# Rotary embedding and attention scores: a sixth load by GpSimd that leaves out four DMA engines, and fewer signals to TensorE

## The chip, the cores and the metric

The kernel runs on one core of one Trainium2 chip. The metric is the device time of an execution in microseconds (us). A core has five instruction streams: TensorE (PE, with its weight loads shown apart as PEld), VectorE (DVE), ScalarE (ACT), GpSimd (POOL) and SyncE (SP), and sixteen DMA engines, numbered 0 to 15 here, which carry every transfer between device memory and on-chip memory. A transfer is issued by SyncE, ScalarE or GpSimd and is spread over several of the sixteen by rows.

## The reference

Two inputs q and k of 16 batches, 512 positions, 16 heads and 64 numbers (32 MB each in fp32) are turned by a rotary embedding, and then all scores of a head are computed. The output has 16 x 512 x 16 x 512 numbers, 256 MB.

```python
q1, q2 = q[..., :half_dim], q[..., half_dim:]
q_rot = np.concatenate([q1 * cos_q - q2 * sin_q, q1 * sin_q + q2 * cos_q], axis=-1)
...
scores = np.einsum('bshd,bthd->bsht', q_rot, k_rot)
```

## The kernel before

A batch of q or k is one tile of 128 partitions: partition p holds positions 4p to 4p+3, which is one contiguous row of 16 KB, so a batch is 128 rows and 2 MB. There are two tiles for q and two for k (`ins`), used in turn. The work goes in 64 steps i (L394 for the first batch, L424 for the others); step i makes the scores of 128 positions of batch i // 4 against all 512 keys: eight pairs of heads, each two matmuls into one of three PSUM tiles `ps` (`scores`, L318), a copy by ScalarE into one of three stage buffers `st` of 4 MB, and one store of 4 MB by SyncE when the eight are there. Between them, TensorE transposes the next q and k parts into two PSUM tiles (`transposed`, L283), and VectorE does the rotary products (`rope_slot`, L251): sines, cosines, sum.

All order is written out by hand in a `Plan` (L11). For every operation it works out which semaphores its engine has to wait for. TensorE does not wait itself: each group of matmuls has a **relay** (L77), an instruction of GpSimd that waits for all that the group needs and then adds one to a semaphore of TensorE's (`emit_plain`, L465 to L476); the group waits for that count (`emit_group`, L487). A relay whose waits are all known already has none and is a bare signal (L475). TensorE's steps 4 to 59 are a loop of two steps (`emit_pe`, L492), whose semaphore is set back by the number of groups at the end of each step.

Loads: `load` (L215) fetches one batch of q or k. Most are issued by SyncE (L224) as one transfer of 128 rows; they stand in SyncE's queue between the stores. Five are in `RELIEVED` (L180) and go through `load_around` (L191): 120 rows by GpSimd in one transfer, the other 8 rows by GpSimd (for k) or by ScalarE (for q). GpSimd's transfers are put on consecutive engines from a cursor, and small copies into a scratch tile that nobody reads (`move_cursor`, L184) move it on by as many engines as they have rows. The relieved loads begin at engine 5 (`SLOW + 1`) and cover 15 engines, which leaves out engine 4. They stand in GpSimd's stream between the relays: a q load ahead of the first scores of its step (L432), a k load behind its step (L454). An input tile may be overwritten when VectorE's last product of the batch two before is done.

Of the kernel before, what the change touches and what calls it, by code (L numbers as in the profile page):

```python
# [7 lines left out]
PE, ACT, DVE, POOL, SP = "PE", "ACT", "DVE", "POOL", "SP"  # L8

class Plan:  # L11
# [7 lines left out]
    def __init__(self):  # L19
        self.ops = {e: [] for e in (PE, ACT, DVE, POOL, SP)}  # L20
        self.count = {}
        self.known = {e: {} for e in self.ops}
        self.writer = {}
        self.readers = {}
        self.phase = "start"
        self.relays = {}

    def _needs(self, reads, writes):
        need = {}
# [41 lines left out]
    def op(self, engine, emit, reads=(), writes=()):  # L71
        needs = self._needs(reads, writes)
        if engine == PE:
            waits = self._waits(POOL, needs, skip=(PE,))
            lane, n = self.phase, self.relays.get(self.phase, 0) + 1
            self.relays[lane] = n
            self.ops[POOL].append(("relay", waits, lane))  # L77
            for s, v in self.known[POOL].items():
                self.known[PE][s] = max(self.known[PE].get(s, 0), v)
            self.ops[PE].append(("group", (lane, n), emit))  # L80
        else:
            self.ops[engine].append(("op", self._waits(engine, needs), emit))
        self._done(engine, 1, engine, reads, writes)

    def dma(self, engine, lane, emit, reads=(), writes=()):
        waits = self._waits(engine, self._needs(reads, writes))
        self.ops[engine].append(("dma", waits, emit, lane))
        self._done(lane, 16, engine, reads, writes)

    def plain(self, engine, emit):  # L90
        self.ops[engine].append(("plain", [], emit))

    def enter(self, phase):

# [6 lines left out]
def kernel(  # L101
# [8 lines left out]
    nc = tc.nc  # L110
# [6 lines left out]
    P = 128  # L117
    C = S // P
# [3 lines left out]
    E = C * H * D  # L122
# [7 lines left out]
    dram = {  # L130
        "q": q.rearrange("b (p c) h d -> b p c h d", c=C),
        "k": k.rearrange("b (p c) h d -> b p c h d", c=C),
    }
# [7 lines left out]
    scratch = const_pool.tile([P, 96], fp32, name="scratch")  # L141
# [12 lines left out]
    plan = Plan()  # L154
# [5 lines left out]
    def dma(engine, lane, dst, src, reads=(), writes=()):  # L160
        plan.dma(engine, lane, lambda: engines[engine].dma_start(dst, src), reads, writes)  # L161
# [15 lines left out]
    def unit_keys(which, n):  # L177
        return [("unit", which, n, x) for x in range(2)]

    RELIEVED = {("q", 6): 0, ("k", 7): 1, ("q", 11): 2, ("k", 12): 3, ("q", 15): 4}  # L180
    SLOW = 4
    tiny = [0]

    def move_cursor(n):  # L184
        y = tiny[0]
        tiny[0] += 1
        src = bass.AP(q.tensor, 512 * y, [(512, n), (64, 2), (1, 2)])
        dst = scratch[:n, 4 * y : 4 * y + 4].rearrange("p (a b) -> p a b", a=2)
        dma(POOL, "tiny", dst, src, writes=[("scratch", y)])

    def load_around(which, b, t, keys):  # L191
        n, small = 120, E // 8
        x = RELIEVED[which, b]
        d = dram[which][b]

        def pieces(engine, lane, lo, hi, F):
            m = E // F
            src = bass.AP(d.tensor, d.offset + lo * E + E - F, [(E, hi - lo), (-F, m), (1, F)])
            v = t[lo:hi].rearrange("p c e -> p (c e)")
            dst = bass.AP(v.tensor, v.offset + E - F, [v.ap[0], (-F, m), (1, F)])  # L200
            dma(engine, lane, dst, src, writes=keys[lane[-1] == "r"])

        if x == 0:
            plan.plain(POOL, lambda: nc.gpsimd.inc_swdge_sem([], [], mode="reset_dge_cursor"))
        else:
            move_cursor(16 - SLOW)
        if x % 2:
            move_cursor(8)
            pieces(POOL, f"w{which}{b % 2}r", n, P, small)
        move_cursor(SLOW + 1)  # L210
        pieces(POOL, f"w{which}{b % 2}m", 0, n, E // 2)
        if not x % 2:
            pieces(ACT, f"a{which}{b % 2}r", n, P, small)

    def load(which, b):  # L215
        if b >= B:
            return
        t = ins[which][b % 2]
        keys = [[("in", which, b % 2, c, x) for c in range(C)] for x in range(2)]
        if (which, b) in RELIEVED:  # L220
            load_around(which, b, t, keys)
        else:
            dst = t.rearrange("p c (h d) -> p c h d", h=H)
            dma(SP, f"{which}{b % 2}m", dst, dram[which][b], writes=keys[0] + keys[1])  # L224

    def vec(out_ap, a, b, op, reads, writes):
        plan.op(DVE, lambda: nc.vector.tensor_tensor(out_ap, a, b, op=op), reads, writes)  # L227
# [23 lines left out]
    def rope_slot(which, n):  # L251
        c = n % C
        x = ins[which][n // C % 2][:, c]
        r = turned[which]
        cs = cos_t[:, c].unsqueeze(1).to_broadcast((P, 2 * H, HD))
        ss = ss_v[:, c].unsqueeze(1).to_broadcast((P, H, D))
        xs = x.rearrange("p (g j) -> p g j", j=D)
        xc = x.rearrange("p (g j) -> p g j", j=HD)
        x4 = x.rearrange("p (h x j) -> p h x j", x=2, j=HD)
        r4 = r.rearrange("p (h x j) -> p h x j", x=2, j=HD)  # L260
        swapped = bass.AP(r.tensor, r.offset + HD, [r.ap[0], (D, H), (-HD, 2), (1, HD)])
        ss4 = ss.rearrange("p h (x j) -> p h x j", x=2)
        u = [("in", which, n // C % 2, c, x) for x in range(2)]
        t = ("turned", which)

        def cosines():
            vec(xc, xc, cs, mult, [*u, "cos"], u)

        def sines():
            vec(swapped, x4, ss4, mult, [*u, "ss"], [t])  # L270

        def sums():
            vec(r4, x4, r4, add, [*u, t], [t])

        return [sines, cosines, sums]
# [79 lines left out]
    def run(ops):  # L355
        for op in ops:
            op()
# [36 lines left out]
    for i in range(C):  # L394
# [8 lines left out]
        for p in range(HP):  # L403
# [7 lines left out]
            if p in (2, 6):  # L411
                m = max(0, len(dve) - left[p == 6])
# [11 lines left out]
    for i in range(C, NST):  # L424
# [6 lines left out]
        q_ops = rope_slot("q", i + 2) if i + 2 < NST else []  # L431
        if i % C == C - 2 and ("q", i // C + 2) in RELIEVED:  # L432
            load("q", i // C + 2)
# [16 lines left out]
        if i % C == C - 2:  # L450
            if ("q", i // C + 2) not in RELIEVED:
                load("q", i // C + 2)
            if ("k", i // C + 3) in RELIEVED:
                load("k", i // C + 3)  # L454
# [5 lines left out]
    def sem(name):  # L460
        if name not in sems:
            sems[name] = nc.alloc_semaphore(name=f"s_{name}")
        return sems[name]

    def emit_plain(engine):  # L465
        eng = engines[engine]
        for item in plan.ops[engine]:
            kind, waits, fn = item[:3]
            if kind == "relay":
                for s, v in waits[:-1]:  # L470
                    eng.wait_ge(sem(s), v)
                if waits:
                    eng.wait_ge(sem(waits[-1][0]), waits[-1][1]).then_inc(sem(fn), 1)  # L473
                else:
                    eng.sem_inc(sem(fn), 1)  # L475
                continue  # L476
            for s, v in waits[:-1]:
                eng.wait_ge(sem(s), v)
            x = fn()
            if waits:  # L480
                x.wait_op(sem(waits[-1][0]), waits[-1][1], "sem-ge")
            if kind == "op":
                x.then_inc(sem(engine), 1)
            elif kind == "dma":
                x.then_inc(sem(item[3]), 16)

    def emit_group(relay, fn):  # L487
        xs = fn()
        xs[0].wait_op(sem(relay[0]), relay[1], "sem-ge")
        xs[-1].then_inc(sem(PE), 1)  # L490

    def emit_pe():  # L492
        ops = plan.ops[PE]
        turns = [x for x, o in enumerate(ops) if o[0] == "phase"]
        for o in ops[: turns[0]]:
            emit_group(*o[1:])
        nc.tensor.addr_align(256, max_nops=0)
        with nc.tensor.Fori(0, (len(turns) - 1) // UNROLL):
            for x in range(UNROLL):
                mine = ops[turns[x] + 1 : turns[x + 1]]  # L500
                for o in mine:
                    emit_group(*o[1:])
                lane = sem(f"turn{x}")
                nc.tensor.wait_ge(lane, len(mine)).then_inc(lane, -len(mine))
        for o in ops[turns[-1] + 1 :]:
            emit_group(*o[1:])

    with tc.tile_critical(no_gpsimd_drain=True):
        for engine in (SP, ACT, DVE, POOL):
            emit_plain(engine)  # L510
        for x in range(3):
            nc.sync.wait_ge(sem(f"st{x}"), plan.count[f"st{x}"])
        nc.gpsimd.wait_ge(sem("tiny"), plan.count["tiny"])
        nc.gpsimd.drain()
        emit_pe()

# [28 lines left out]
```

## Time and profile before

| | |
|---|---|
| median of 3 runs | 794.82 us (794.64 to 795.95) |
| the profiled execution | 793.15 us, its span 791.4 us |
| TensorE busy | 679.4 us, 86% of the span |
| VectorE, ScalarE busy | 573.9 us (73%), 552.1 us (70%) |
| DMA | 335.90 MB, mean 424 GB/s over the span |
| read, written | 67.24 MB, 268.44 MB |
| GpSimd's transfers | 3.1% of the DMA engines' time |
| stores of 4 MB, issue to landing | 25.4 us (60 of them) |
| relays with a wait, without | 626, 142 |

The span runs from the first to the last instruction. The time of a run lies a little above the span. A busy share is an average over the span; the slices of the page show how it is spread. A transfer's landing is signed off by sixteen records in the trace, one for each DMA engine, whether it carried data or not; the last of them lets the waiting instruction go.

### The profile page before, as it was taken

What the parts mean: (1) busy time and instruction counts of PE and PEld (TensorE: products, weight loads), DVE (VectorE), ACT (ScalarE), POOL (GpSimd) and SP (SyncE); (2) the same over time, 40 slices, a digit from 0 to 9 for tenths busy, and PEclk for the clock granted to TensorE, in tenths of its full rate; (3) what the DMA queues carried; (4) which work ended last, traced back from release to release, by engine and by line L of the source; (5) the groups of instructions that cost most, each with busy time, mean ns of one, the idle gap of its engine ahead of it and who ended that gap; (6) DMA issues with size and microseconds to landing.
All of it is one profiled execution on the core that took longest, in us unless ns stands there. A gap on an engine that the chain in (4) does not pass through costs nothing.

```text
span 791.4 us, 8521 instructions
## 1 busy us (share of the span) xinstructions
PE 679.4 (86%) x3072; PEld 290.4 (37%) x3072; DVE 573.9 (73%) x544; ACT 552.1 (70%) x647; POOL 11.9 (2%) x24
## 2 busy tenths in 40 slices
PE   4988999989978999698897978989889697999960
PEld 2443444333433434243343433334334243334320
DVE  7997898766857788585786767779578584877510
ACT  3978886866847777486684866868667685688770
POOL 0000000000010000000000001000000000000000
PEclk9999999988999999899998999999989998999995
DMA  9999999999999999999999999999999999999996
GB/s 354 421 425 439 428 436 434 421 441 432 428 428 434 427 431 410 442 429 429 433 431 434 431 428 434 428 429 417 440 426 432 437 428 428 435 432 428 435 434 270
DMA packets 19086, 335.90 MB, mean 424 GB/s; under 512 B 2376, under 2 KB 3656, under 8 KB 4936
## 3 DMA queue, kind: packets, MB, share of 16 engines
q1 hardware_dynamic: 16288, 324.61, 95.8%
q0 software_dynamic: 1872, 10.10, 3.1%
q10 hardware_dynamic: 904, 0.98, 0.4%
q14 instruction: 18, 0.15, 0.0%
q8 instruction: 4, 0.07, 0.0%
HBM read 67.24 MB, written 268.44 MB: 424 GB/s over the span
## 4 chain that ended last, share of the span: by engine, by line
DMA 48%; PE 29%; ACT 11%; DVE 7%; issue 0%; ACTq 0%; POOLq 0%; DVEq 0%; SPq 0%
DMA out_dram<-st 48%; PE ps L336 23%; ACT st L281 11%; PE bank L293 6%; DVE st L227 3%; DVE qr L227 2%; DVE kr L227 2%; DVE k_sb L227 1%; ACT kN L281 1%; DMA st<-in_k_dram 0%; DVE kT L279 0%; DVE q_sb L227 0%; ACTq L161 0%; POOLq L473 0%; ACTq L541 0%
## 5 line engine op out<-in xcount | busy, mean ns | idle before, releaser
L281 ACT COPY st<-ps 128x1024 f32<-128x1024 f32 x512 | 495.1, 1033 | 201.6 <-DMA out_dram<-st 132.2
L336 PE MATMUL ps<-kT,qT 64*128 64x512 f32 x1920 | 506.0, 646 | 71.7 <-POOLq L473 69.4
L336 PEld LDWEIGHTS ps<-kT,qT 64*128 64x128 f32 x1920 | 167.8, 194 | 252.8 <-POOLq L473 165.8
L279 DVE COPY qT<-bank 128x512 f32<-128x512 f32 x118 | 81.5, 691 | 115.0 <-PE bank L293 114.8
L227 DVE TENSOR_TENSOR kr<-k_sb,ss_t 128x1024 f32<-128x1024 f32 x60 | 73.2, 1220 | 27.1 <-PE bank L293 24.3
L293 PEld LDWEIGHTS bank<-ident,qr 128*128 128x128 f32 x480 | 52.6, 145 | 99.0 <-issue 66.2
L293 PEld LDWEIGHTS bank<-ident,kr 128*128 128x128 f32 x480 | 50.5, 141 | 94.7 <-issue 49.3
L293 PE MATMUL bank<-ident,qr 128*128 128x128 f32 x480 | 82.2, 296 | 1.3 <-POOLq L473 1.2
L293 PE MATMUL bank<-ident,kr 128*128 128x128 f32 x480 | 79.0, 288 | 2.1 <-POOLq L473 2.1
L281 ACT COPY kN<-bank 128x512 f32<-128x512 f32 x120 | 72.7, 608 | 8.5 <-PE bank L293 8.4
L227 DVE TENSOR_TENSOR qr<-q_sb,qr 128x1024 f32<-128x1024 f32 x60 | 73.5, 1225 | 2.0
L227 DVE TENSOR_TENSOR kr<-k_sb,kr 128x1024 f32<-128x1024 f32 x60 | 73.5, 1225 | 2.0
L227 DVE TENSOR_TENSOR q_sb<-q_sb,cos_t 128x1024 f32<-128x1024 f32 x60 | 73.5, 1225 | 2.0
L227 DVE TENSOR_TENSOR k_sb<-k_sb,cos_t 128x1024 f32<-128x1024 f32 x60 | 73.0, 1216 | 0.2
L227 DVE TENSOR_TENSOR qr<-q_sb,ss_t 128x1024 f32<-128x1024 f32 x60 | 72.9, 1216 | 0.0
L279 DVE COPY kT<-kN 128x2048 f32<-128x2048 f32 x28 | 34.3, 1226 | 30.4 <-PE ps L336 18.6
L293 PE MATMUL bank<-ident,st 128*128 128x128 f32 x64 | 10.7, 317 | 12.2 <-POOLq L473 12.2
L336 PE MATMUL ps<-kN,qT 64*128 64x512 f32 x64 | 16.7, 643 | 0.0
L336 PE MATMUL ps<-kN,st 64*128 64x512 f32 x64 | 16.3, 616 | 0.0
L161 POOL DMA_DIRECT2D scratch<-in_q_dram x11 | 6.3, 575 | 631.5 <-DVE qT L279 613.8
L293 PEld LDWEIGHTS bank<-ident,st 128*128 128x128 f32 x64 | 8.3, 161 | 17.4 <-POOLq L473 17.4
L227 DVE TENSOR_TENSOR qr<-st,ss_t 128x1024 f32<-128x1024 f32 x8 | 9.8, 1221 | 5.4 <-DMA st<-in_k_dram 5.3
(19 smaller groups left out, 50.6 us busy)
## 6 DMA issues: line engine op xcount, KB each, us to landing
out_dram<-st SPq DMA_DIRECT2D x60, 4096.0 KB, 25.4
k_sb<-in_k_dram SPq DMA_DIRECT2D x13, 2048.0 KB, 30.0
q_sb<-in_q_dram SPq DMA_DIRECT2D x12, 2048.0 KB, 28.7
out_dram<-st SPq DMA_DIRECT2D x16, 1024.0 KB, 14.0
q_sb<-in_q_dram POOLq DMA_DIRECT2D x3, 1920.0 KB, 28.2
k_sb<-in_k_dram POOLq DMA_DIRECT2D x2, 1920.0 KB, 50.8
st<-in_k_dram SPq DMA_DIRECT2D x1, 1536.0 KB, 8.9
st<-in_q_dram SPq DMA_DIRECT2D x1, 1536.0 KB, 11.9
```

Source lines behind the costliest of these rows:

```text
L161: plan.dma(engine, lane, lambda: engines[engine].dma_start(dst, src), reads, writes)
L227: plan.op(DVE, lambda: nc.vector.tensor_tensor(out_ap, a, b, op=op), reads, writes)
L279: plan.op(DVE, lambda: nc.vector.tensor_copy(out=dst, in_=src), reads, writes)
L281: plan.op(ACT, lambda: nc.scalar.copy(out=dst, in_=src), reads, writes)
L293: return [nc.tensor.transpose(bank[:, x, :], srcs[x], ident) for x in range(4)]
L336: nc.tensor.matmul(out=ps[:, r, :], lhsT=lhs[64 * r : 64 * r + 64, :], rhs=rhs[64 * r : 64 * r + 64, :], start=True, stop=True,)
```

## The change

Two things are changed.

First, q of batch 13 joins the relieved loads, with another split (`MORE`): 24 rows, then 96 rows, both by GpSimd and counted by the code as twelve engines from engine 5 on (5 to 15 and 0), then 8 rows by GpSimd from engine 8 on. Its rows have three keys and three semaphores instead of two. The copies that move the cursor are now worked out from where the code believes the cursor to be (`cursor[0]`), each transfer adding the number of engines that is written beside it: 15, 12 or 8. So the other relieved loads are led by one or two small copies instead of up to three.

Second, the plan notes whether GpSimd has waited for anything since its last relay (`heard`). A relay that has no wait, and before which GpSimd heard nothing new, is dropped (`thin`), and its group on TensorE waits for no count. The counts of the others are numbered anew. Where a relay has several waits, two go into one instruction.

```diff
+            self.ops[POOL].append(("relay", waits, lane, n, bool(waits) or self.heard))
+            self.heard = False
...
+    def thin(self):
+        needed = {o[2:4] for o in self.ops[POOL] if o[0] == "relay" and o[4]}
+        rank, count = {}, {}
+        for place in sorted(needed):
+            lane = place[0]
+            count[lane] = rank[place] = count.get(lane, 0) + 1
+        self.ops[POOL] = [o for o in self.ops[POOL] if o[0] != "relay" or o[2:4] in needed]
+        self.ops[PE] = [
+            ("group", (o[1][0], rank.get(o[1])), o[2]) if o[0] == "group" else o for o in self.ops[PE]
+        ]
+        return count
...
-    RELIEVED = {("q", 6): 0, ("k", 7): 1, ("q", 11): 2, ("k", 12): 3, ("q", 15): 4}
     SLOW = 4
+    ONE, MORE = 15, 12
+    RELIEVED = {("q", 6): ONE, ("k", 7): ONE, ("q", 11): ONE, ("k", 12): ONE, ("q", 13): MORE, ("q", 15): ONE}
+    cursor = [None, 0]
+
+    def move_cursor(to):
+        if cursor[0] is None:
+            plan.plain(POOL, lambda: nc.gpsimd.inc_swdge_sem([], [], mode="reset_dge_cursor"))
+            cursor[0] = 0
+        n, y = (to - cursor[0]) % 16, cursor[1]
+        if n:
+            src = bass.AP(q.tensor, 512 * y, [(512, n), (64, 2), (1, 2)])
+            dst = scratch[:n, 4 * y : 4 * y + 4].rearrange("p (a b) -> p a b", a=2)
+            dma(POOL, "tiny", dst, src, writes=[("scratch", y)])
+            cursor[:] = [to, y + 1]
...
+        def pieces(engine, lane, lo, hi, F, written, first=None, n=0):
...
+            if engine == POOL:
+                move_cursor(first)
+                cursor[0] = (first + n) % 16
+            dma(engine, lane, dst, src, writes=written)
+
+        x = b % 2
+        if RELIEVED[which, b] == MORE:
+            pieces(POOL, f"w{which}{x}r", 96, 120, wide, keys[1], SLOW + 1, MORE)
+            pieces(POOL, f"w{which}{x}m", 0, 96, wide, keys[0], SLOW + 1, MORE)
+            pieces(POOL, f"w{which}{x}s", 120, P, small, keys[2], 8, 8)
+        elif which == "k":
+            pieces(POOL, f"w{which}{x}r", 120, P, small, keys[1] + keys[2], 8, 8)
+            pieces(POOL, f"w{which}{x}m", 0, 120, wide, keys[0], SLOW + 1, ONE)
+        else:
+            pieces(POOL, f"w{which}{x}m", 0, 120, wide, keys[0], SLOW + 1, ONE)
+            pieces(ACT, f"a{which}{x}r", 120, P, small, keys[1] + keys[2])
...
     def emit_group(relay, fn):
         xs = fn()
-        xs[0].wait_op(sem(relay[0]), relay[1], "sem-ge")
+        if relay[1]:
+            xs[0].wait_op(sem(relay[0]), relay[1], "sem-ge")
         xs[-1].then_inc(sem(PE), 1)
...
-                nc.tensor.wait_ge(lane, len(mine)).then_inc(lane, -len(mine))
+                n = count[f"turn{x}"]
+                nc.tensor.wait_ge(lane, n).then_inc(lane, -n)
```

The new `load_around` gives GpSimd's pieces of q of batch 13 with `wide` = 2048 numbers and `small` = 512 numbers as the length of one run in a row; rows are the slowest dimension on both sides of every one of these transfers.

More of the change, by code (lines that the diff above doesn't have):

```diff
@@ L76, in op @@
             self.relays[lane] = n
-            self.ops[POOL].append(("relay", waits, lane))
+            self.ops[POOL].append(("relay", waits, lane, n, bool(waits) or self.heard))
+            self.heard = False
             for s, v in self.known[POOL].items():
@@ L81, in op @@
         else:
-            self.ops[engine].append(("op", self._waits(engine, needs), emit))
+            waits = self._waits(engine, needs)
+            self.heard |= engine == POOL and bool(waits)
+            self.ops[engine].append(("op", waits, emit))
         self._done(engine, 1, engine, reads, writes)
@@ L86, in dma @@
         waits = self._waits(engine, self._needs(reads, writes))
+        self.heard |= engine == POOL and bool(waits)
         self.ops[engine].append(("dma", waits, emit, lane))
@@ L178, in unit_keys @@
         return [("unit", which, n, x) for x in range(2)]
-    RELIEVED = {("q", 6): 0, ("k", 7): 1, ("q", 11): 2, ("k", 12): 3, ("q", 15): 4}
     SLOW = 4
[L182 to L189, printed above, removed]
+    ONE, MORE = 15, 12
[11 more added lines that the diff above has]
+            cursor[:] = [to, y + 1]
     def load_around(which, b, t, keys):
-        n, small = 120, E // 8
-        x = RELIEVED[which, b]
+        wide, small = E // 2, E // 8
         d = dram[which][b]
-        def pieces(engine, lane, lo, hi, F):
+        def pieces(engine, lane, lo, hi, F, written, first=None, n=0):
             m = E // F
@@ L200, in pieces @@
             dst = bass.AP(v.tensor, v.offset + E - F, [v.ap[0], (-F, m), (1, F)])
-            dma(engine, lane, dst, src, writes=keys[lane[-1] == "r"])
-        if x == 0:
-            plan.plain(POOL, lambda: nc.gpsimd.inc_swdge_sem([], [], mode="reset_dge_cursor"))
-        else:
[L206 to L213, printed above, removed]
+            if engine == POOL:
[10 more added lines that the diff above has]
+            pieces(POOL, f"w{which}{x}m", 0, 120, wide, keys[0], SLOW + 1, ONE)
+        else:
+            pieces(POOL, f"w{which}{x}m", 0, 120, wide, keys[0], SLOW + 1, ONE)
+            pieces(ACT, f"a{which}{x}r", 120, P, small, keys[1] + keys[2])
     def load(which, b):
@@ L218, in load @@
         t = ins[which][b % 2]
-        keys = [[("in", which, b % 2, c, x) for c in range(C)] for x in range(2)]
+        keys = [[("in", which, b % 2, c, x) for c in range(C)] for x in range(3)]
         if (which, b) in RELIEVED:
@@ L223, in load @@
             dst = t.rearrange("p c (h d) -> p c h d", h=H)
-            dma(SP, f"{which}{b % 2}m", dst, dram[which][b], writes=keys[0] + keys[1])
+            dma(SP, f"{which}{b % 2}m", dst, dram[which][b], writes=keys[0] + keys[1] + keys[2])
     def vec(out_ap, a, b, op, reads, writes):
@@ L262, in rope_slot @@
         ss4 = ss.rearrange("p h (x j) -> p h x j", x=2)
-        u = [("in", which, n // C % 2, c, x) for x in range(2)]
+        u = [("in", which, n // C % 2, c, x) for x in range(3)]
         t = ("turned", which)
@@ L469, in emit_plain @@
             if kind == "relay":
[L470 to L475, printed above, removed]
+                if not waits:
+                    eng.sem_inc(sem(fn), 1)
+                while waits:
+                    now, waits = waits[:2], waits[2:]
+                    x = eng.wait_ge(sem(now[0][0]), now[0][1])
+                    if len(now) == 2:
+                        x.wait_op(sem(now[1][0]), now[1][1], "sem-ge")
+                    if not waits:
+                        x.then_inc(sem(fn), 1)
                 continue
@@ L488, in emit_group, with emit_pe @@
         xs = fn()
-        xs[0].wait_op(sem(relay[0]), relay[1], "sem-ge")
+        if relay[1]:
+            xs[0].wait_op(sem(relay[0]), relay[1], "sem-ge")
         xs[-1].then_inc(sem(PE), 1)
-    def emit_pe():
+    def emit_pe(count):
         ops = plan.ops[PE]
@@ L503, in emit_pe @@
                 lane = sem(f"turn{x}")
-                nc.tensor.wait_ge(lane, len(mine)).then_inc(lane, -len(mine))
+                n = count[f"turn{x}"]
+                nc.tensor.wait_ge(lane, n).then_inc(lane, -n)
         for o in ops[turns[-1] + 1 :]:
             emit_group(*o[1:])
+    relayed = plan.thin()
     with tc.tile_critical(no_gpsimd_drain=True):
@@ L514 @@
         nc.gpsimd.drain()
-        emit_pe()
+        emit_pe(relayed)
 _INS = ['q', 'k', 'cos', 'sin']
```

## The prediction

> **What bounds the kernel now.** I read the page's slices first, then the chain, then the end of the span in short stretches, then what GpSimd waits for. From the page's second part (40 slices, busy share in tenths, and GB/s) and its fourth (the chain that ended last):
>
> ```profile
> DMA  9999999999999999999999999999999999999996
> GB/s 354 421 425 439 428 436 434 421 441 432 428 428 434 427 431 410 442 429 429 433 431 434 431 428 434 428 429 417 440 426 432 437 428 428 435 432 428 435 434 270
> DMA 48%; PE 29%; ACT 11%; DVE 7%; issue 0%; ACTq 0%; POOLq 0%; DVEq 0%; SPq 0%
> ```
>
> The DMA engines are full from the first slice to the last but one, which no compute engine is (TensorE 86%). The chain's 29% of TensorE misleads: it runs under a full queue. Summed over the trace's packet records, the sixteen engines are idle for 0.6 us per engine before 780 us, 0.5 of it in the first 10 us. So waits of TensorE, ScalarE or GpSimd cost nothing as long as the queue holds work. Only the last slice is not full. Its stretches (columns: busy time of PE, PEld, DVE, ACT, POOL, granted clock, DMA share, GB/s):
>
> ```profile
> 770.00:780.00 10.00, 0.00 (x0) 0.00 (x0) 0.00 (x0) 0.00 (x0) 0.00 (x0) 0.57 1.02 439
> 780.00:782.00 2.00, 0.00 (x0) 0.00 (x0) 0.00 (x0) 0.00 (x0) 0.00 (x0) 0.50 0.80 344
> 782.00:784.00 2.00, 0.00 (x0) 0.00 (x0) 0.00 (x0) 0.00 (x0) 0.00 (x0) 0.50 0.57 246
> 784.00:786.00 2.00, 0.00 (x0) 0.00 (x0) 0.00 (x0) 0.00 (x0) 0.00 (x0) 0.50 0.42 180
> 786.00:788.00 2.00, 0.00 (x0) 0.00 (x0) 0.00 (x0) 0.00 (x0) 0.00 (x0) 0.50 0.11 49
> 788.00:791.40 3.40, 0.00 (x0) 0.00 (x0) 0.00 (x0) 0.00 (x0) 0.00 (x0) 0.50 0.02 10
> ```
>
> All compute is over; the sixteen engines run out one after another, and the last one sets the time. Which one? Every transfer leaves sixteen landing records. Those of the last store, in us behind the first (781.85), are 0, 0.33, 0.34, 0.43, 1.57, 1.62, 1.85, 1.92, 1.96, 3.05, 4.70, 4.98, 5.40, 5.60, 7.64, 8.15. Their mean is 3.1: bytes moved between engines can win at most 8.15 - 3.1 = 5 us.
>
> To name the engines I followed packets: on one engine the next packet starts 3 to 4 ns before the last one's end. The 8-row pieces that ScalarE issues touch eight engines (I number them 0 to 7), those of GpSimd the other eight, 8 to 15. Of the two small copies at 656 us, with twelve and five rows, exactly one engine carries both, so the second begins where the first came round: 4 to 15, then 0 to 4. That sorts the list: **engine 4** 8.15; engines 0 to 3: 1.85, 5.40, 5.60, 7.64 (I take 1.85 for engine 0, the one that no 8 KB instruction fetch was seen to hit); 5 to 7: 1.92, 1.96, 4.98; 8 to 15: 0, 0.33, 0.34, 0.43, 1.57, 1.62, 3.05, 4.70. Engine 4 is last for a reason: until 767 us its 32 KB packets take a median 1255 ns, the others' 1213, so it loses 0.33 us per 4 MB store. Only the five loads by GpSimd, which leave it out, hold it back:
>
> ```profile
> q_sb<-in_q_dram POOLq DMA_DIRECT2D x3, 1920.0 KB, 28.2
> k_sb<-in_k_dram POOLq DMA_DIRECT2D x2, 1920.0 KB, 50.8
> scratch<-in_q_dram POOLq DMA_DIRECT2D x5, 0.1 KB, 7.6
> scratch<-in_q_dram POOLq DMA_DIRECT2D x4, 0.2 KB, 13.3
> ```
>
> In the landings of each of these five loads one engine comes 3.8 to 5.9 us ahead of fifteen: the one with nothing to carry. The scratch rows are the small copies that turn GpSimd's cursor.
>
> **The change, part by part.**
>
> *Signals left out.* The trace has 142 signals without a wait:
>
> ```profile
> L475 POOLq EVENT_SEMAPHORE  x142: 17/17/17, 9.3 to 758.7; - x142
> PEld ps L336 <- POOLq L475: 2.3, 9, 0.5
> POOL q_sb L161 <- DVE qr L227: 17.3, 3, 5.9
> ```
>
> At most these 142 go, 142 x 17 ns = 2.4 us of GpSimd's sequencer, and TensorE waited 2.3 us for them. The DMA queue hides both: 0. Without that cover it would be 2.3 us. Putting two waits into one instruction changes nothing: 112 of the 626 waiting signals already carry two. Fewer instructions are fewer fetches: 18 packets of 8 KB (0.31 us each) for the 2255 instructions of all engines but TensorE is 65 bytes each, so 142 spare about 1.1 packets, 0.35 us on one engine. I take 0 and keep -0.35 for the range. Small copies go from 11 to 10, with packets of 9 ns: 0.
>
> *The load moved to GpSimd.* q of batch 13 leaves SyncE's queue (issued at 575.08) and goes into GpSimd's before step 46, so it waits for VectorE's last product of step 45 with TensorE's signals of step 46 queued behind it. The row is the same kind of load at step 54: copies at 656.07, 5.68 us of waiting, load at 662.87. Step 45's store left SyncE at 559.11 where step 53's left at 658.80, so the copies would come near 556.4 and the load near 563.2, with three pieces (0.75, 0.75, 0.59) and three copies (0.56 each): 3.8 us more at most. TensorE stands for 5.7 to 9.5 us. What hides it: store 46 waits anyway for its buffer, whose last store lands at 565.3; and from its issue at 574.70 to its first landing, 592.90, lie 18.2 us, of which 9.7 are its own service (one store to the next at the end, 772.20 to 781.85). So 8.5 us are queue. Price 0; with all of 9.5 uncovered, 1.0 us dry. The removed issue on SyncE (0.85) and VectorE's waits for three lanes in place of one (17 ns each, as a signal of GpSimd's) are 0 as well.
>
> *Where the bytes go.* This decides. A row is 16 KB, 0.61 us (611 ns in one packet, 2 x 309 in two). Before, q of batch 13 put eight rows on every engine. The new pieces have 24, 96 and 8 rows, and the code counts the first two as twelve engines each. The trace has no GpSimd transfer of 96 rows. It shows 120 rows on 15 engines, 12 on 12, 8 on 8, 5 on 5, and SyncE's 128 rows on 16: each time the largest number up to 16 that divides the rows; for 120 not 12 or 10, though both divide. By these rows 24 goes on 12, but **96 goes on 16**, six rows each. That is the value I take; the other bound is the code's 12, eight rows each.
>
> The Trainium skill, "DMA: Bandwidth & Descriptors", section "Why a DMA increments its semaphore by 16 and not by 1", says the same of the rule: the largest k up to 16 that divides both sides' slowest dimension, all engines at k = 16, otherwise k consecutive ones from a cursor. The trace agrees on 120, 12, 8 and 5; no run here shows 96. By that page the sum is the one that follows; by the code's count it is the first rival's.
>
> With 16, the count slips. After the 24 rows (engines 5 to 15 and 0) the cursor is at 1; a copy of four brings it to 5; the 96 rows go everywhere and leave it at 5, while the code believes 1. Its copy of seven leads to 12, not 8: the 8 rows fall on 12 to 15 and 0 to 3, and the cursor ends at 4, not 0. Before the last load (q of batch 15) the code moves by five, to 9, not 5: its 15 engines are 9 to 15 and 0 to 7. **It leaves out engine 8 and gives engine 4 eight rows.**
>
> Sum for engine 4: batch 13, 6 - 8 = -2 rows, -1.2; batch 15, 8 instead of 0, +4.9; 8.15 - 1.2 + 4.9 = 11.85, so +3.7 us. No other comes near: 7.64 - 0.6 = 7.0 (engines 1 to 3, 7 rows); 4.70 + 0.6 = 5.3 (12 to 15, 9 rows).
>
> *Slow reads behind such loads.* In the first SyncE load after each pair of GpSimd loads, 16 KB reads took up to 1.72 us instead of 0.61 (300 to 308 us; again 541 to 555); mean lateness rose by 0.6 and 0.5 us, the latest engine's by 1.8 and 0.1. The k load at 590.84 would now follow one. Whether it pays is open: 0 taken (a single load comes before it, not a pair), 1.8 kept for the range.
>
> The profiled execution took 793.15 us with a span of 791.4, 1.75 around it; the median of the runs is 794.82, 1.67 higher. Span 791.4 + 3.7 = 795.1; on the median 794.82 + 3.7 = **798.5 us**. The runs lie from 794.64 to 795.95, so the case's own range is 797.2 (less the fetch and a spread of 0.9) to 800.3 (plus 1.8).
>
> **Rivals.**
>
> *The 96 rows do use twelve engines.* Engines 1 to 4 get nothing: 7.64, 5.60, 5.40 and 8.15 fall by 4.9, to 3.3 and less. Engines 8 to 15 get 11 rows, +1.8: 4.70 becomes 6.5; engines 5 to 7 get 10: 4.98 becomes 6.2. The end moves from 8.15 to 6.5, -1.6 us: 793.2. For it: it is just what would relieve the four latest. Against: the 120-row rows.
>
> *Sixteen engines, but the cursor comes out where the code believes.* The last load then spares engine 4: 8.15 - 1.2 = 6.9, 793.6. Against: nothing shows a transfer on sixteen moving the cursor by twelve.
>
> *Twelve engines, and step 46 runs the queue dry.* 1.0 us dry and 0.6 of slow reads give the gain back: 794.8. It decides only once TensorE's stand exceeds 8.5 us; the three waits behind VectorE were at most 5.9 each.
>
> *Engine 4 does not matter.* The same page of the Trainium skill (section "Latency and other measured facts") says engines 7 and 15 are usually the slower, with SWDGE's rings as the guess. Worked out here: if 4.98 and 8.15 were swapped, engine 7 at 8.15 would get 6 + 2 rows and its usual eight at batch 15, and the time would stay 794.8. The trace disagrees: the engine with 1255 ns packets carries rows of both small copies, and it is slow long before GpSimd's first load (from some 50 us).
>
> **How the numbers follow.** Forecast 0.71; twelve engines 0.18; cursor right 0.04; dry queue 0.05; engine 7 0.02. A measurement tells some 0.2% from no change, 1.6 us: below 793.2 faster, above 796.4 slower. Twelve engines lie on that bound: 0.11 faster, 0.07 same; cursor right 0.02 and 0.02; the last two same. Faster 0.13, same 0.16, slower 0.71. The forecast's own range holds some 0.64; to reach 0.8 the range goes down over the middle cases to 793.1.
>
> **What would show it.** In the landings of q of batch 13's 96-row piece, four early engines mean twelve, none means sixteen. In the last load, the engine left out must be one with 1213 ns packets. The last store's landings should end 11.8 behind the first, by the engine with 1255 ns packets, with the next near 7, and DMA still full before 780 us. I am wrong if four engines come early, or if an idle stretch of the DMA opens near 575 to 600 us.

## The result and the profile after

| | before | after |
|---|---|---|
| median | 794.73 us (4 runs, 793.30 to 795.95) | 802.73 us (4 runs, 801.93 to 804.19) |
| ratio, with its 95% interval | | 1.0103 (1.0079 to 1.0128) |
| the profiled execution, its span | 793.15, 791.4 us | 804.19, 802.4 us |
| idle time of one DMA engine, mean of the sixteen | 5.5 us | 12.5 us |
| GpSimd's transfers, share of the DMA engines | 3.1% | 3.7% |

The kernel became slower, as forecast, but by 8.0 us and not by 3.7, and 802.73 us lies above the stated range. The two profiled executions lie 11.0 us apart, more than the medians: the one of before is low among its runs, the one of after is the highest of its four.

First the slices and the chain of the changed kernel's page, to be held against those of before:

```profile
DMA  9999999999999999999999999999999999999994
GB/s 346 421 426 432 440 387 425 429 429 441 423 432 430 426 438 412 433 437 429 431 428 440 433 428 425 422 431 423 432 426 411 428 430 434 419 407 422 436 425 178
DMA 53%; PE 24%; ACT 12%; DVE 6%; issue 1%; POOL 0%; ACTq 0%; POOLq 0%; DVEq 0%; SPq 0%
```

The last slice holds 178 GB/s where it held 270, slices 35 and 36 (some 680 to 720 us) fall to 419 and 407, and slice 6 (100 to 120 us) to 387. Those are the three places where most of the time went; a fourth, smaller one is slice 31 (some 600 to 620 us, behind the sixth load), 411 where before has 432. The end, in short stretches (some of the rows; columns as before, the last two are DMA share and GB/s):

```profile
780.00:782.00 2.00, 0.00 (x0) 0.00 (x0) 0.00 (x0) 0.00 (x0) 0.00 (x0) 0.56 1.22 524
788.00:790.00 2.00, 0.00 (x0) 0.00 (x0) 0.00 (x0) 0.00 (x0) 0.00 (x0) 0.50 0.76 328
790.00:792.00 2.00, 0.00 (x0) 0.00 (x0) 0.00 (x0) 0.00 (x0) 0.00 (x0) 0.50 0.19 82
792.00:794.00 2.00, 0.00 (x0) 0.00 (x0) 0.00 (x0) 0.00 (x0) 0.00 (x0) 0.50 0.08 33
794.00:796.00 2.00, 0.00 (x0) 0.00 (x0) 0.00 (x0) 0.00 (x0) 0.00 (x0) 0.50 0.08 33
796.00:798.00 2.00, 0.00 (x0) 0.00 (x0) 0.00 (x0) 0.00 (x0) 0.00 (x0) 0.50 0.04 16
798.00:800.00 2.00, 0.00 (x0) 0.00 (x0) 0.00 (x0) 0.00 (x0) 0.00 (x0) 0.50 0.08 33
```

Two packets of 32 KB in 2 us make 33 GB/s, one makes 16. So from 792.8 us on a single engine works, for 8 us. In the landings of the last store fifteen engines come within 2.55 us of the first (790.26), and engine 4 comes 10.79 behind it. Before, the sixteen were strung out over 8.15 us with a mean of 3.1. Engine 4 no longer is the last of a crowd: it alone carries more.

How long it had been so shows in the stores from 640 us on. These are from the landing records of the changed kernel (us; the last columns are the latest and the next latest engine behind the first):

```
issued   first landing   latest   next
647.22   660.42          11.10    6.39
657.23   674.98          15.21    8.17
667.24   687.24          14.67    8.36
683.55   699.37          12.54    6.46
699.57   710.46          11.48    5.02
710.36   721.24          10.73    3.91
720.37   731.25          10.73    3.55
730.40   741.29          10.68    3.16
```

The latest engine was 15 us behind at 675 us. A stage buffer is free only when the last of its sixteen records is there, so the others then began to wait for engine 4, and the stores fell into its pace: 10.0 us from one to the next (721.24 to 731.25), eight packets of 1255 ns, where before they came every 9.7, eight of 1213 ns. That is the dip at 680 to 720. It shows as missing GB/s while TensorE is nearly full, in the changed kernel:

```profile
690.00:700.00 10.00, 8.67 (x34) 3.62 (x36) 5.56 (x6) 8.60 (x10) 0.00 (x0) 0.83 0.94 400
720.00:730.00 10.00, 10.00 (x50) 4.34 (x48) 8.44 (x9) 8.37 (x11) 0.00 (x0) 1.00 0.99 426
730.00:740.00 10.00, 10.00 (x50) 4.33 (x48) 6.74 (x7) 8.38 (x11) 0.00 (x0) 1.00 0.97 416
```

and in the kernel before, in the same stretches:

```profile
690.00:700.00 10.00, 9.12 (x44) 3.78 (x44) 7.56 (x8) 7.96 (x10) 0.00 (x0) 1.00 1.01 436
720.00:730.00 10.00, 10.00 (x50) 4.41 (x50) 6.76 (x7) 8.59 (x11) 0.00 (x0) 1.00 1.02 440
730.00:740.00 10.00, 9.81 (x46) 4.01 (x46) 6.46 (x8) 7.92 (x9) 0.00 (x0) 1.00 1.01 434
```

Summed over the packet records, the 11.0 us of the profiled pair come out so. Idle time per engine behind 780 us rose by 4.6 (4.9 to 9.5), before it by 2.4 (1.9 of it between 690 and 750 us). Packets that took longer than the usual 1213, 611 or 309 ns cost 3.8 us per engine more (3.8 to 7.6), 1.8 of it at 100 to 120 us, long before the first load that the change touches; such a patch stands there in some executions of the kernels below and not in others. Together 10.8. The idle time fits the late engine; that the slow packets have to do with the change is not shown.

Where did engine 4 fall behind? Followed packet by packet, it is +1.1 us against before at 470 us, +8.4 at 550, +7.3 at 656, +11.1 at 700, and +11.05 at the end. **The largest step, 7.3 us, falls on the time of q of batch 11 and k of batch 12**, two loads that were relieved before as well, and the next, 3.8 us, on q of batch 15. Over the time of the new load 1.1 us came back. In that first stretch engine 4 carries no 8 KB packet for GpSimd before, and 32 of them after: eight rows of each of the two loads.

### The profile page after: what moved, and what is told of

Read it like the earlier page. It is cut to its first block, busy times and chain, and to the rows that moved or that the text cites. A ratio compares the mean times of both kernels' runs of the same rounds, so it can differ in the third digit from the quotient of the medians.

```text
span 802.4 us, 8390 instructions
## 1 busy us (share of the span) xinstructions
PE 680.4 (85%) x3072; PEld 291.8 (36%) x3072; DVE 573.3 (71%) x544; ACT 551.6 (69%) x647; POOL 13.4 (2%) x26
## 4 chain that ended last, share of the span: by engine, by line
DMA 53%; PE 24%; ACT 12%; DVE 6%; issue 1%; POOL 0%; ACTq 0%; POOLq 0%; DVEq 0%; SPq 0%
DMA out_dram<-st 53%; PE ps L361 19%; ACT st L306 11%; PE bank L318 6%; DVE st L252 2%; DVE kr L252 1%; DVE qr L252 1%; ACT kN L306 1%; DVE k_sb L252 1%; DMA st<-in_k_dram 0%; DVE kT L304 0%; DVE q_sb L252 0%; DVE qT L304 0%; POOL scratch L179 0%; ACTq L179 0%
```

## The experiments

**What was open.** The prediction had one cause of harm, the 96 rows counted as twelve engines, and it comes too late to reach q 11. Something had already turned the cursor wrongly before. What is new before q 11 is a small copy of **one row**: the code believes the cursor at 4, wants 5, and copies one row (its source is 1 x 2 x 2 numbers). In the trace that copy leaves two packets of 8 bytes and some thirty empty ones of 4 bytes, so two engines carry it and not one. A first theory was that it moves the cursor by two. The rival was that the new load is what costs.

The first four kernels, in one session (the kernel before: 795.34 us).

**The signals alone.** The loads and small copies of before, with the thinned signals.

```diff
-    RELIEVED = {("q", 6): ONE, ("k", 7): ONE, ("q", 11): ONE, ("k", 12): ONE, ("q", 13): MORE, ("q", 15): ONE}
+    RELIEVED = {("q", 6): 0, ("k", 7): 1, ("q", 11): 2, ("k", 12): 3, ("q", 15): 4}
...
```

> The kernel before with the signals left out, its loads untouched. Theory (the whole loss is in where GpSimd's loads fall on the DMA engines): 794.7 us, within 0.8 of before, and the last landing of the last store is still engine 4's, some 8 us behind the first. Rival (the thinner signals let TensorE run into the DMA or starve it): 2 us or more to either side.

Measured: 794.77 us in 12 runs (793.30 to 802.79; all but that one below 796.5), ratio 1.0002 (0.9982 to 1.0022). The last store's latest landing is 7.5 us behind its first. The signals neither cost nor gain anything that can be told.

**The one-row copy replaced.** Wherever the cursor should move by one, copies of 8 and 9 rows move it by 17, which is the same. The 96 rows stay.

```diff
-        if n:
-            src = bass.AP(q.tensor, 512 * y, [(512, n), (64, 2), (1, 2)])
+        for m in (8, 9) if n == 1 else (n,) if n else ():
+            src = bass.AP(q.tensor, 512 * y, [(512, m), (64, 2), (1, 2)])
...
```

> The changed kernel with its one-row copies replaced by two copies of 8 and 9 rows, which also move the cursor by one (17 modulo 16); the 96-row piece stays. Theory (two faults: a one-row copy goes on two engines and moves the cursor by two; 96 rows go on sixteen engines): the loads of q 11 and k 12 leave out engine 4 again, so only the last load is misplaced (it leaves out engine 8): 797.3 to 798.5 us, 2.6 to 3.8 over before. Rival (the 96-row piece alone is to blame, as the prediction had it): the time stays at 802.7. Rival (the one-row copies alone): 793.1.

Measured: 798.18 us in 12 runs (797.02 to 800.15), ratio 1.0034 (1.0021 to 1.0047). This is the kernel that the prediction had in mind. The end of its span:

```profile
786.00:788.00 2.00, 0.00 (x0) 0.00 (x0) 0.00 (x0) 0.00 (x0) 0.00 (x0) 0.50 0.38 164
788.00:790.00 2.00, 0.00 (x0) 0.00 (x0) 0.00 (x0) 0.00 (x0) 0.00 (x0) 0.50 0.27 115
790.00:792.00 2.00, 0.00 (x0) 0.00 (x0) 0.00 (x0) 0.00 (x0) 0.00 (x0) 0.50 0.08 33
792.00:794.00 2.00, 0.00 (x0) 0.00 (x0) 0.00 (x0) 0.00 (x0) 0.00 (x0) 0.50 0.04 16
```

The engines thin out over several us, and one stands alone for 4.7 us at the end, 10.56 behind the first with the next at 5.82. Of the 96-row piece no four landings come ahead of the rest (0, 0.03, 0.84, 1.10, 2.03 and so on): it is on sixteen engines. So with the one-row copies mended some 5 of the 8 us are gone.

**Both replaced.** The same, with 108 and 12 rows in place of 96 and 24; 108 is divided by twelve and by nothing between it and sixteen.

```diff
-            pieces(POOL, f"w{which}{x}r", 96, 120, wide, keys[1], SLOW + 1, MORE)
-            pieces(POOL, f"w{which}{x}m", 0, 96, wide, keys[0], SLOW + 1, MORE)
+            pieces(POOL, f"w{which}{x}r", 108, 120, wide, keys[1], SLOW + 1, MORE)
+            pieces(POOL, f"w{which}{x}m", 0, 108, wide, keys[0], SLOW + 1, MORE)
```

> As the run before, and q of batch 13 in pieces of 108, 12 and 8 rows, of which 108 and 12 can only go on twelve engines. Theory: all loads fall where the code counts them, four engines land early in the 108-row piece, the end is 6.5 us behind the first landing: 793.1 us, 1.6 below before. Rival (a sixth load by GpSimd costs by its stall of TensorE or its slow reads): 795 to 797.

Measured: 796.57 us in 12 runs (792.78 to 799.10), ratio 1.0012 (0.9993 to 1.0030): no difference that can be told. The 108 rows do show four early engines (0, 0.53, 2.03, 2.14, then 6.95 and more). The load now does what the change says and still wins nothing. In this profiled execution (798.79 us) the latest landing is 7.72 us behind the first, hardly less than before, the next is at 4.10, and the slow patch at 100 to 120 us is there (1.7 us per engine). It was taken once more below.

**The one-row copies alone.** The changed kernel with q of batch 13 back on SyncE. One-row copies stand before q 11 and q 15.

```diff
-    RELIEVED = {("q", 6): ONE, ("k", 7): ONE, ("q", 11): ONE, ("k", 12): ONE, ("q", 13): MORE, ("q", 15): ONE}
+    RELIEVED = {("q", 6): ONE, ("k", 7): ONE, ("q", 11): ONE, ("k", 12): ONE, ("q", 15): ONE}
```

> The changed kernel with q of batch 13 back in SyncE's queue; the one-row copies stay. Theory: q 11 and k 12 leave out engine 5 and q 15 leaves out engine 6, so engine 4 carries 24 rows more than before: 11 to 12 us on it, 804 to 807 us. Rival (only the 96-row piece is wrong): 794.7.

Measured: 802.85 us in 6 runs (802.33 to 804.90), ratio 1.0096 (1.0076 to 1.0117), a little under the 804 to 807 that were expected. The rival falls: without any new load the whole loss is there. It also shows that the two faults do not add up: the 96 rows alone cost 2.8 us (798.18 against 795.34), the one-row copies alone 7.5, and both together no more than the one-row copies alone. By the table below, both put the same eight rows of q 15 on engine 4. Two of its stretches:

```profile
690.00:700.00 10.00, 9.15 (x34) 3.93 (x36) 5.48 (x6) 8.33 (x10) 0.00 (x0) 0.71 0.69 296
792.00:794.00 2.00, 0.00 (x0) 0.00 (x0) 0.00 (x0) 0.00 (x0) 0.00 (x0) 0.50 0.08 33
```

At 690 to 700 us the DMA engines have 0.69 of their time filled, since the stage buffers wait for one engine, 16.6 to 18.0 us behind at 672 to 684; at the end it is alone, 10.39 behind the first and the next at 1.94.

The next four, in one session (the kernel before: 795.36 us).

**The kernel before, and both replaced, once more**, for a second pair of profiles.

> The kernel before once more, for a second profile of it: if its time is near 796, slow reads stand at 100 to 120 us; if near 794, they do not. The last landing is engine 4's, 7.5 to 8.2 us behind the first, in both cases.

> The run with both faults mended once more, for a second profile. Theory (executions differ by slow reads at 100 to 120 us, which the first profile of it had and that of before had not): either the slow reads at 100 to 120 us are there and the span is near 797, or they are not and it is near 792.

Measured: 793.56 us (span 791.8) and 792.74 us (span 791.0). Neither has the slow patch at 100 to 120 us, as was expected of times this low. The end of the latter:

```profile
784.00:786.00 2.00, 0.00 (x0) 0.00 (x0) 0.00 (x0) 0.00 (x0) 0.00 (x0) 0.50 0.76 328
786.00:788.00 2.00, 0.00 (x0) 0.00 (x0) 0.00 (x0) 0.00 (x0) 0.00 (x0) 0.50 0.27 115
788.00:790.00 2.00, 0.00 (x0) 0.00 (x0) 0.00 (x0) 0.00 (x0) 0.00 (x0) 0.50 0.04 16
```

In this execution the relief works: the latest landing is 4.07 behind the first where the kernel before has 8.17, and idle time per engine falls from 6.0 to 3.4 us. But the mean landing comes 1.8 us later (785.53 + 1.5 against 782.24 + 3.0), because between 580 and 620 us, behind the sixth load, packets cost 1.6 us per engine more than usual; there the kernel before has nothing. 2.6 us less skew (latest over mean: 5.2 to 2.6) and 1.8 us more work leave -0.8 us of span. The first profile of the same kernel ended 7.72 behind, so how much of the end is won differs from one execution to the next, and what decides it stays open.

**The sixth load behind its step.** Both replaced, and q of batch 13 issued behind step 46, so that none of TensorE's signals is queued behind its wait.

```diff
-        if i % C == C - 2 and ("q", i // C + 2) in RELIEVED:
+        if i % C == C - 2 and RELIEVED.get(("q", i // C + 2)) == ONE:
...
-            if ("q", i // C + 2) not in RELIEVED:
+            if RELIEVED.get(("q", i // C + 2)) != ONE:
```

> Both faults mended, and the sixth load stands behind step 46 in GpSimd's stream instead of ahead of it, so that no signal to TensorE waits behind VectorE. Theory (the sixth load's price is the stall of TensorE that it brings): the slow reads at 550 to 620 us shrink to those of before and the time falls by 1 to 1.5 us against the run with both faults mended, to 795.2. Rival (the price lies in the load on GpSimd's queue itself): the slow packets behind it stay, and the time with them, 796.6.

Measured: 795.22 us in 12 runs (792.78 to 797.67), ratio 1.0000 (0.9987 to 1.0013). By time this can't be told from the kernel that stalls TensorE (1.0012, 0.9993 to 1.0030). The time of 795.22 us is the theory's own figure, but the kernel before took 795.36 us beside it, so that says little. The profile says more: the slow patch behind the load stays (0.41, 0.36 and 1.25 us per engine at 590 to 620), as the rival had it, and the latest landing is 4.33 behind. The patch does not come from TensorE's stand; whether the stand costs something besides, these runs can't tell.

**Relief without a sixth load.** The kernel before's five loads, with the 8 rows that ScalarE puts on engines 0 to 7 given to GpSimd, on 8 to 15; signals thinned, and copies of 8 and 9 rows for "one".

```diff
...
-        elif which == "k":
+        else:
             pieces(POOL, f"w{which}{x}r", 120, P, small, keys[1] + keys[2], 8, 8)
             pieces(POOL, f"w{which}{x}m", 0, 120, wide, keys[0], SLOW + 1, ONE)
-        else:
-            pieces(POOL, f"w{which}{x}m", 0, 120, wide, keys[0], SLOW + 1, ONE)
-            pieces(ACT, f"a{which}{x}r", 120, P, small, keys[1] + keys[2])
```

> The kernel before with the thinner signals, five relieved loads as before, but the 8-row pieces of q 6, 11 and 15 go by GpSimd to engines 8 to 15 instead of by ScalarE to 0 to 7. Theory (the end is set by the latest engine alone, and nothing else is paid where no load is added): engine 4 loses three rows, 8.15 - 1.8 = 6.3 behind the first, engines 8 to 15 gain them, 4.70 + 1.8 = 6.5: 1.6 us below before. Rival (each further GpSimd transfer ahead of a step costs as the sixth load did): no faster than before.

Measured: 794.55 us in 12 runs (792.28 to 802.10; all but that one below 796.1), ratio 1.0001 (0.9981 to 1.0021). The latest landing moved to 6.44 behind the first, as the bytes say, but slow reads at 300 and 550 us took 1.1 and 0.6 us per engine, where the repeat of the kernel before has 0.6 and 0.2. No version here beats the kernel before.

**What does a one-row copy do to the cursor?** Two more kernels (the kernel before: 795.31 us). The first is the one with both replaced, but with the copies for "one" of 1 and 15 rows in place of 8 and 9: right if a one-row copy moves by two (2 + 15 = 17), two short if it moves by none.

```diff
-        for m in (8, 9) if n == 1 else (n,) if n else ():
+        for m in (1, 15) if n == 1 else (n,) if n else ():
```

> Both faults mended as before, but where the cursor has to move by one, a one-row copy and a 15-row copy stand instead of 8 and 9 rows. Theory (a one-row copy goes on two engines and moves the cursor by two, 2 + 15 = 17): the loads fall as in the run with 8 and 9 rows, in the landings of q 11 one engine comes 3 us or more ahead of the others, and the time is that run's, 795 to 797. Rival (a one-row copy moves the cursor by one or not at all): every load behind it is one or two engines off, engine 4 carries rows in all of them, and the time is 800 or more.

Measured: 805.23 us in 4 runs (803.89 to 805.88), ratio 1.0119 (1.0091 to 1.0148). The theory of two falls.

**No relief at all.** All loads by SyncE, to see what the relief is worth and whether slow patches need GpSimd's loads.

```diff
-    RELIEVED = {("q", 6): ONE, ("k", 7): ONE, ("q", 11): ONE, ("k", 12): ONE, ("q", 13): MORE, ("q", 15): ONE}
+    RELIEVED = {}
...
```

> The changed kernel with no relieved loads: all loads by SyncE, on sixteen engines; the signals stay thinned. Theory of the end: engine 4 carries 40 rows more than in the kernel before, less 3 that ScalarE put there, 22.6 us, less some of the 3 us by which its stores are slowed while GpSimd loads run: 805 to 815 us, with engine 4 more than 15 us behind the rest. Theory of the slow packets (they come with GpSimd's loads): none of the stretches of slow packets that stand at 260 to 310 and 510 to 560 us. Rival: they are as before.

Measured: 805.69 us, one execution, span 803.9. The time is near the low edge of what was expected; the last store's latest landing is 8.9 us behind and not more than 15, because here too the others wait for the latest engine, which was 14.5 behind at 729 us:

```profile
720.00:730.00 10.00, 6.94 (x22) 2.98 (x24) 3.40 (x4) 5.75 (x7) 0.00 (x0) 0.69 0.89 383
730.00:740.00 10.00, 10.00 (x48) 4.22 (x44) 8.06 (x8) 8.08 (x10) 0.00 (x0) 0.97 0.66 282
```

And slow patches are there without a single load by GpSimd: 0.9 us per engine at 500 to 520, 1.2 at 550 to 570, 1.8 at 590 to 620. That they come with such loads is not borne out; where they come from stays open.

The last two kernels (the kernel before: 795.53 us) tell "none" from all else. **One row, then seventeen**: the copies for "one" are of 1, 8 and 9 rows, with the 108 rows; right only if the one-row copy moves nothing.

```diff
-        for m in (8, 9) if n == 1 else (n,) if n else ():
+        for m in (1, 8, 9) if n == 1 else (n,) if n else ():
```

> Both faults mended; where the cursor has to move by one, a one-row copy stands ahead of the copies of 8 and 9 rows. Theory, formed after the run with one and 15 rows (a one-row copy leaves the cursor where it is, though it goes on two engines): the loads fall as with 8 and 9 rows alone, 795 to 797 us, and in the landings of q 11 one engine comes 3 us or more ahead. Rival (it moves the cursor by any other number): engine 4 carries rows again, 800 us or more.

**The one-row copies left out.** The changed kernel, believing that the cursor moved by one but without the copy.

```diff
-        if n:
+        if n > 1:
...
+        elif n:
+            cursor[0] = to
```

> The changed kernel without its two one-row copies; the code's count still goes on by one. Theory (a one-row copy leaves the cursor where it is): the time is that of the changed kernel, 802.7, with engine 4 last by 10 to 11 us. Rival (the one-row copy moves the cursor by some number): the loads fall on other engines than in the changed kernel, and the end differs from it by 2 us or more, or the landings of q 11 to q 15 show other patterns.

Measured: 794.89 us in 10 runs (793.33 to 800.40), ratio 0.9999 (0.9978 to 1.0021), and 804.43 us in 4 runs, ratio 1.0114 (1.0092 to 1.0137). With the one-row copy added to a right count nothing changes, and in the landings of q 11 one engine comes 4.07 us ahead of the others; with it taken from the changed kernel the loss stays, and the last two stores end with the latest engine 10.79 us behind the first, the very figure of the changed kernel, and the next at 1.8. **A one-row copy leaves the cursor where it is.** With that the changed kernel's engines can be written down (the landings and the small copies that engine 4 carries agree with each line):

```
                        the code believes         what happens
q 11   120 rows         5 to 15, 0 to 3           4 to 15, 0 to 2    leaves out 3
k 12   8 rows           8 to 15                   7 to 14
       120 rows         5 to 15, 0 to 3           4 to 15, 0 to 2    leaves out 3
q 13   24 rows          5 to 15, 0                3 to 14
       96 rows          5 to 15, 0                all sixteen
       8 rows           8 to 15                   10 to 15, 0, 1
q 15   120 rows         5 to 15, 0 to 3           7 to 15, 0 to 5    leaves out 6
```

Engine 4 gets eight rows of each of the three loads that were to spare it, and of q 13 its usual eight (2 + 6): 24 rows more than before. The Trainium skill, "DMA: Bandwidth & Descriptors", section "Why a DMA increments its semaphore by 16 and not by 1", takes the slowest dimension that is not of size 1. For a one-row copy that is the 2, and the trace's two 8-byte packets agree with two engines; that the cursor then moves by two, which its account of consecutive engines from a round-robin cursor would suggest, is what the copies of 1 and 15 rows disproved.

## Why the prediction was wrong, step by step

*What bounds the kernel*: right. The DMA engines are full and the latest engine sets the end. Every kernel that gave engine 4 more rows became slower. Those that spared it further ended 4.07 to 7.72 us behind the first landing (these two are one kernel in two executions), against 7.52 to 8.17 with the loads of before.

*Signals*: right, 0 as far as can be told (794.77 against 795.34). The instruction fetches that should fall by about 1.1 fell by one:

```profile
q14 instruction: 17, 0.14, 0.0%
```

*TensorE's stand at step 46*: it came, at the length that was forecast, and the DMA queue hid it. GpSimd's waits for VectorE's last products went from 17.3 us over three to 19.6 over four. From the waits, the timelines of POOL and PE, and the short stretches of the changed kernel:

```profile
POOL q_sb L179 <- DVE qr L252: 19.6, 4, 6.3
569.66 0.63 POOL L179 DMA_DIRECT2D q_sb<-in_q_dram  x1 [5.59 <-DVE qr L252]
571.79 3.77 PE L361 MATMUL ps<-kT,qT 64*128 64x512 f32 x8 [6.81 <-POOLq L499]
560.00:570.00 10.00, 4.99 (x26) 2.10 (x22) 7.76 (x8) 5.66 (x7) 0.90 (x2) 0.93 0.99 424
570.00:580.00 10.00, 8.21 (x31) 3.36 (x32) 1.23 (x1) 5.11 (x7) 2.70 (x5) 0.73 1.01 434
```

The sum hides the new wait, since that of q 6 shrank from 5.90 to 2.05 us. The new one is 5.59 us (forecast 5.68), and TensorE stood for 6.81 us (forecast 5.7 to 9.5), with the DMA engines filled to 0.99 and 1.01 of their time. With the load where it stalls nothing, the time is the same within the intervals.

*96 rows on sixteen engines*: right. No four early landings, twelve packets for engine 4 in that piece (six rows of 16 KB as 8 KB runs), and four early ones as soon as it is 108 rows. Its size about held: the kernel in which only this is wrong took 798.18 us, +2.8 us and 1.0034 (1.0021 to 1.0047) times the kernel before, that is 1.7 to 3.7 us, with the forecast of +3.7 at the upper edge. Its last landings were 10.56 and 5.82 behind the first where 11.85 and 7.0 were worked out. In the changed kernel itself, however, this fault adds nothing that can be told: without it, with the one-row copies alone, the time is 802.85 us against 802.73. That the kernel became slower, as forecast, was thus in part luck: another fault had already made it so.

*The step that failed* is one half of a sentence: "Small copies go from 11 to 10, with packets of 9 ns: 0." The copies were counted and priced, and what they do was taken from the code. The prediction started the cursor of q 13 at 5 because the code says so, and never asked whether q 11 and k 12, which both kernels relieve, still got the right engines. They did not: their cursor was led by copies of 12, 8 and 5 rows before; now a single row stands before q 11 and before q 13, a form that the trace of before does not have. That adds two loads on engine 4, and turns the third, q 15, in another way than worked out (it leaves out 6, not 8, which for engine 4 is the same eight rows). Two of the signs that the prediction had named did fail: DMA was to be full before 780 us, and the idle time there rose by 2.4 us; the next landing was to be near 7 us behind the first, and was at 2.55. The bound that this step asked for could be had: a copy of a form never seen moves the cursor by its rows or it does not, and "not" puts 2 x 8 rows x 0.61 = 9.8 us more on engine 4.

*The size of that term* is not fully the rows' either. 24 rows are 14.7 us; engine 4 ended 11.05 us later. When it was left out of q 11 and k 12, its 56 store packets at 470 to 550 us took 5.4 us more than 1213 ns each, which is 3.1 over its own usual 1255; carrying the rows, 52 packets took 2.0 more, no more than is usual for it. So being spared 9.8 us of rows saved engine 4 some 7. Why its stores run slower when it is left out stays open.

*Rivals*: the twelve engines, 793.2, were made true by the 108 rows. The skew halved in one execution and hardly changed in another, and the time did not fall (1.0012, 0.9993 to 1.0030; with the extra one-row copies 0.9999). In the execution where it halved, the slow patch behind the load, for which the prediction took 0 and kept 1.8, took 1.6 us and gave most of the gain back; since 1.8 us of such packets stand at 590 to 620 in the kernel without any load by GpSimd too, it is not shown that the load brings them. The cursor did not come out where the code believes: with the one-row copies mended the last store ended 10.56 behind, not 6.9. The queue did not run dry at step 46 (0.99 and 1.01 above). Nothing here speaks for engine 7.

## What to carry to other kernels

A shared cursor that nobody can read makes every small step before a transfer part of its cost: when an edit changes how such a state is advanced, follow it through all transfers behind the edit, and most of all through those that seem unchanged. If the trace has no instruction of exactly the new form (one row, 96 rows), its effect is an unknown with two ends, not a rule applied. Where sixteen engines share each transfer, look at the latest landing and the next latest: here one engine far behind alone (10.79, next 2.55) was a fault in the spread, while the kernel before ends in a long string (8.15, 7.64, 5.60).

## What the runs showed of the hardware

- A GpSimd copy whose outer dimension is one row went to two engines by its inner dimension of two, and left the cursor in place (794.89 us with it added to a right count, 804.43 with it removed from a wrong one), while the places of the loads fit copies of 4, 5, 7, 8, 9 and 12 rows that moved it by their rows.
- An engine that a load leaves out is not wholly spared: beside GpSimd's loads, at 470 to 550 us, its stores took 5.4 us over 1213 ns a packet (3.1 over its own usual 1255), against 2.0 (none over its own usual) where it carried its share.
- 16 KB reads slow down in patches of some 10 to 20 us (0.5 to 1.8 us per engine), at places that differ between executions and kernels, also without any load by GpSimd. The cause is open.
- One late engine holds back fifteen: with three stage buffers, a lag that had grown to 14 to 18 us fell back to 8 to 11 us while the stores went at the late engine's pace (one every 10.0 us in place of 9.7).
